# Norm column inside the mixers' first segment, and late weight splits queued behind the turned softmax tiles

## The chip, the cores and the metric

The kernel runs on one core of one Trainium2 chip. A core has five engines with a queue each: TensorE (PE; its weight loads are listed as PEld), VectorE (DVE), ScalarE (ACT), GpSimd (POOL) and SyncE (SP), whose queue only issues DMA here. An engine takes its instructions in the order in which they stand in its queue; instructions of different engines are held together by semaphores. The metric is the device time of one execution in microseconds (us). Before the change the median of three runs is 984.71 us (984.63 to 985.41).

## The reference: what is computed

A decoder trunk of two layers over 256 tokens of width 1024, all in float32. Each layer is a half SwiGLU step (FFN, inner width 2816), an attention mixer with 16 heads of 64, and another half SwiGLU step. Every step reads an RMS-normalised copy of the stream:

```python
y = xf * lax.rsqrt(jnp.mean(xf * xf, axis=-1, keepdims=True) + RMS_EPS)
return (y * g.astype(jnp.float32)).astype(x.dtype)
```

Mixer a projects q, k and v, rotates 16 of 64 columns of each q and k head, adds up three dilated window patterns (in the kernel one mask of logarithms of counts), and projects the result with `a_w_o`. Mixer b does causal attention with its own q projection and keys and values that were projected from another norm of the stream after layer 0; with 256 tokens there is a single block of keys. The output is a final RMS norm.

## The kernel before

**Precision.** Every float32 product is made of three products of float32r halves. A weight tile `raw` is rounded by ACT (`wh`) and the remainder is subtracted by DVE (`wl`); I call this pair a split. Splits are made for 128x1024 elements at a time, into pools of eight buffers; `raw` has four buffers, so a load on SP's queue waits until both halves of an older tile are split. Activations are split in the same manner (`parts_of`).

**Norms.** The stream lies transposed in `hT` (feature rows, token columns). A `Norm` makes two things. `scale` gives gain-scaled, split blocks `x`, which products can use at once. The factor per token comes later: `square` lets ACT square the eight blocks and POOL add them up in `ss`; `finish` sums over the partitions with four small PE products (`col`, L238), adds epsilon on DVE (`v`, L240) and takes the power -0.5 on POOL (`c`, L242). The result is one column per token tile (two tiles of 128 tokens), and it is applied when a projection leaves its accumulator.

**A mixer** (L704 to L786) works in segments. A segment is one block of 512 projected columns for both token tiles: for the first four weight rows tile 0 then tile 1, for the last four the same, three products for each row (L184, L186, L188). `evacuate` scales a finished accumulator by the norm's column (ACT, L752), lets DVE rotate it (L622 to L625) and, when q and k of a group of heads are there, has PE turn them (L741, `qt`). In mixer a the norm's column isn't there when the first segment ends; in mixer b the first segment (k and v) uses a norm whose column is long known, and the second (q) one whose column isn't. For those, both tiles are evacuated after the segment's last product:

```python
if norm.col is None:
    norm.finish()
    for t in range(NT):
        evacuate(i, t, norm.col[t], acs[t], parts)
```

Attention goes by pairs of heads, 0 to 7: scores (PE L643, DVE L651), softmax (ACT L657, POOL L664), turn of the softmax (PE L669 `pt`, split into `pT` by ACT L98 and DVE L94), values (PE L683 and L685 `po`), and evacuation of those (`o`, `oT`). The output projection (`out_t`, L580) multiplies with the pairs as they come: five rows in a main loop of 24 products each, the last three held back and done together at the end.

**Order.** A small agenda (L258) decides at which point of PE's work a step is written down: `after(wait, ...)` puts a step `wait` us of estimated work later. Weights of a mixer come through `Pieces` (L284): asking for one piece rounds all up to four pieces further on (`LEAD`), and DVE's subtraction is written one piece later. Finally the framework's scheduler sorts the queues by its own cost model, within the dependencies; so a split written down late can still be put early in ACT's and DVE's queues, whenever its raw tile and a free buffer are there by that model.

**The FFN after a mixer** loads its first unit of gate and up weights (1 MB each) as four splits, `wh_f_g` and `wh_f_u` (L158, L159). They need nothing of the mixer's result, so they stand among the mixer's last steps in the queues.

Of the kernel before, what the change touches and what calls it, by code (L numbers as in the profile page):

```python
# [29 lines left out]
LEAD = 4  # L30
# [36 lines left out]
def trunk(ctx: ExitStack, tc: tile.TileContext, a: dict, out: bass.AP):  # L67
    nc = tc.nc
# [69 lines left out]
    def late_constants():  # L138
        nc.sync.dma_start(rot, a["rot"].rearrange("t p c n -> p t c n"))
        nc.sync.dma_start(masks, a["masks"].rearrange("i p n -> p i n"))  # L140
        nc.sync.dma_start(gfin, a["final_norm"].rearrange("(o d) -> o d", o=1).to_broadcast([P, D]))


    def unit(name, k, n, srcs):

        raw = rawp.tile([P, k, n], F32, tag="raw", name=f"raw_{name}")
        for dst, src in srcs:
            nc.sync.dma_start(raw if dst is None else raw[:, :, dst], src)
        return pieces_of(name, raw, k, n)

    def pieces_of(name, raw, k, n):
        pieces = []
        for j in range(0, k, 1024 // n):
            kk = min(1024 // n, k - j)
            wh = wp.tile([P, kk, n], F32R, tag="wh", name=f"wh_{name}_{j}")
            wl = wp.tile([P, kk, n], F32R, tag="wl", name=f"wl_{name}_{j}")
            r = raw[:, j:j + kk, :]
            nc.scalar.activation(wh, r, AF.Copy)  # L158
            nc.vector.tensor_sub(wl, r, wh.bitcast(F32))  # L159
            for i in range(kk):  # L160
                pieces.append((wh[:, i, :], wl[:, i, :]))
        return pieces
# [15 lines left out]
    def rows(w, k0, k, c0, n):  # L178
        return w[k0 * P:(k0 + k) * P, c0:c0 + n].rearrange("(k p) n -> p k n", p=P)
# [104 lines left out]
    class Pieces:  # L284
# [29 lines left out]
                    self.rest.pop(0)()  # L314

        def __getitem__(self, i):
            self.split(i + LEAD)
            return self.parts[i]


# [16 lines left out]
        parts_of(hi, lo, flat(q), later=rest.append)  # L337
        return rest

    def ffn_blocks(name, wg, wu, norm, first=None, beside=(), sums=None):  # L340

        blocks, pairs, rest = [], {}, []

        def both(f, pair):
            acs = [acc(f"{name}_{n}{f}") for n in "gu"]
            cols = slice(f % 2 * P, (f % 2 + 1) * P)
            products_t(acs, [[(wh[:, cols], wl[:, cols]) for wh, wl in w] for w in pair], norm.x, True, True)
            return acs  # L350

        def close(f, gate, up):
            g = joined(gate, f"{name}_g{f}")
            nc.vector.tensor_mul(g, g, norm.row)  # L354
# [12 lines left out]
            parts_of(x[:, 0], x[:, 1], prod)  # L367
            while rest:
                rest.pop(0)()
            if prod is not g and f % 2:  # L370
                rest.extend(quarter_sums(pairs.pop(pair), *sums[pair], f"{name}_{f}"))
            blocks.append(x)

        done = []

        def close_all():
            if done and norm.row is None:
                norm.spread()
            for args in done:
                close(*args)  # L380
            done.clear()

        for f in range(0, KF, 2):
            if f == 0 and first is not None:
                ws = opening(wg, wu, first)
            else:
                ws = zip(*[unit(f"{name}_{n}{f}", KD, S, [(None, rows(w, 0, KD, f * P, S))])
                           for n, w in (("g", wg), ("u", wu))])
# [24 lines left out]
        return blocks  # L413
# [12 lines left out]
                                for j in range(2))  # L426
        return sums

    def ffn(name, layer, which, norm, after, first=None, beside=(), homes=("kx4", "kx6", "qkh", "qkh")):
        wg, wu, wd = (a[f"ffn{which}_w_{n}"][layer] for n in ("gate", "up", "down"))  # L430
        sums = left_sums(homes)
        blocks = ffn_blocks(name, wg, wu, norm, first, beside, sums)
        if which == 1:
            table(AF.Exp, blocks[-1][:, 0, 0:1].bitcast(F32))
        down(f"{name}_d", wd, blocks, sums, after)
# [141 lines left out]
                part(t, slice(512 + S, 1024), True)  # L577
            after(t)

    def out_t(name, pieces, base, blocks, norm, tail=3):  # L580

        accs = [acc(f"ot_{name}_{i}") for i in range(KD // 2)]

# [8 lines left out]
                nc.tensor.matmul(ac, wl[:, d], hi, start=False, stop=k == KD - 1 and j == 1)  # L592

        for k in range(KD - tail):
            ws = pieces[base + k][0]
            while len(blocks) <= k:
                yield None
            for i in range(KD // 2):
                step(i, k, ws)
                yield 0.72  # L600
# [26 lines left out]
    def attention(agenda, operands, mask, name, blocks):  # L627
# [38 lines left out]
        def turn(p, i):  # L666
            tr = trt(f"pt_{name}{p}_{i}")[:, :3 * P]
            for n in range(3):
                nc.tensor.transpose(tr[:, n * P:(n + 1) * P], sms[p, i][:, n * P:(n + 1) * P], ident)  # L669
            pT = pTs[p, i] = pp.tile([P, 2, 3 * P], F32R, tag="pT", name=f"pT_{name}{p}_{i}")  # L670
            parts_of(pT[:, 0], pT[:, 1], tr, later=agenda.soon)

        def values(p):
            g, b = divmod(p, HG // 2)
# [26 lines left out]

        return scores, turn, values

    def mixer(name, segs, plan, wo, mask, after):  # L704

# [17 lines left out]
        for norm in {id(norm): norm for norm, _, _ in segs}.values():  # L723
            for i in range(len(norm.late)):
                agenda.after(1.5 + 0.5 * i, lambda norm=norm: norm.late.pop(0)())
        scores, turn, values = attention(agenda, lambda g: (qks[g], vss.get(g)), mask, name, blocks)

        def turns(p):
# [18 lines left out]
        def evacuate(i, t, r, ac, parts):  # L747
# [38 lines left out]
        agenda.run(out_t(f"{name}o", pieces, base, blocks, after))  # L786


    def first(k, n):
# [21 lines left out]
    def ending(at):  # L811
# [28 lines left out]
    blocks = ffn_blocks("f21", a["ffn2_w_gate"][1], a["ffn2_w_up"][1], n6, beside=[lambda: None] + turns, sums=sums)  # L840

    parts = [[], []]
    outs = [[None, None] for t in range(NT)]
# [63 lines left out]
```

## Time and profile before

| | |
|---|---|
| median of three runs | 984.71 us |
| the profiled execution | 984.39 us |
| its span, first to last instruction | 982.6 us |
| mean granted TensorE clock | 0.999 |
| busy: PE, DVE, ACT, POOL | 968.3, 813.0, 613.8, 289.6 us |
| mixer a in the span, about | 190 to 310 us |
| mixer b in the span, about | 675 to 790 us |

The profile's page gives busy time by engine. Other answers of the trace list instructions in order of time: start, length, engine, line, operation, output and inputs, size, count, and in brackets the idle time of the engine just before it and what ended that. Equal neighbours are merged into one row with their count; the ends of matmuls are modelled, so the next product can start before the last has ended in the list. Buffer numbers are left out of names: `wl_qka` stands for several tiles.

### The profile page before, as it was taken

What the parts mean: (1) busy time and instruction counts of PE and PEld (TensorE: products, weight loads), DVE (VectorE), ACT (ScalarE), POOL (GpSimd) and SP (SyncE); (2) the same over time, 40 slices, a digit from 0 to 9 for tenths busy, and PEclk for the clock granted to TensorE, in tenths of its full rate; (3) what the DMA queues carried; (4) which work ended last, traced back from release to release, by engine and by line L of the source; (5) the groups of instructions that cost most, each with busy time, mean ns of one, the idle gap of its engine ahead of it and who ended that gap; (6) DMA issues with size and microseconds to landing.
All of it is one profiled execution on the core that took longest, in us unless ns stands there. A gap on an engine that the chain in (4) does not pass through costs nothing.

```text
span 982.6 us, 14865 instructions
## 1 busy us (share of the span) xinstructions
PE 968.3 (99%) x5391; PEld 832.8 (85%) x5391; DVE 813.0 (83%) x1383; ACT 613.8 (62%) x1131; POOL 289.6 (29%) x242
## 2 busy tenths in 40 slices
PE   8999999999999999999999999999999999999997
PEld 6888888878889888888888888888788998888886
DVE  7988899887878788889898888987678778888995
ACT  7656657567776566556576655656577766666561
POOL 3211246132342211146032121612142422112461
PEclk9999999999999999999999999999999999999999
DMA  9876636664443565545755555483744345565351
GB/s 317 256 238 186 197 132 217 223 203 155 132 129 106 179 201 178 185 158 210 256 168 176 172 182 205 171 283 109 248 131 129 101 158 170 177 204 180 129 171 43
DMA packets 126857, 176.00 MB, mean 179 GB/s; under 512 B 3392, under 2 KB 106304, under 8 KB 126784
## 3 DMA queue, kind: packets, MB, share of 16 engines
q1 hardware_dynamic: 125936, 174.01, 54.4%
q10 hardware_dynamic: 848, 1.05, 0.3%
q8 instruction: 42, 0.69, 0.3%
q14 instruction: 31, 0.25, 0.1%
HBM read 173.99 MB, written 1.05 MB: 178 GB/s over the span
## 4 chain that ended last, share of the span: by engine, by line
PE 68%; ACT 2%; DVE 2%; issue 1%; POOL 0%; POOLq 0%; ACTq 0%; DVEq 0%
PE f_g L195 12%; PE f_u L195 12%; PE f_u L198 6%; PE f_g L198 6%; PE dn_f_d L188 5%; PE dn_f_d L186 5%; PE dn_f_d L184 5%; PE dn_f_d_m L188 1%; PE dn_f_d_m L186 1%; PE dn_f_d_m L184 1%; PE q_b L184 1%; PE q_b L188 1%; PE q_b L186 1%; PE ot_ao L592 1%; PE ot_ao L590 1%; PE kv_b L184 1%
## 5 line engine op out<-in xcount | busy, mean ns | idle before, releaser
L357 POOL TENSOR_TENSOR j_f_u<-j_f_u,r_n 128x256 f32<-128x256 f32 x88 | 92.3, 1051 | 360.9 <-DVE j_f_u L325 338.1
L195 PE MATMUL f_g<-x_n,wh_f_g 128*128 128x512 f32 x688 | 180.5, 394 | 0.0
L195 PE MATMUL f_u<-x_n,wh_f_u 128*128 128x512 f32 x688 | 177.2, 390 | 0.0
L195 PEld LDWEIGHTS f_u<-x_n,wh_f_u 128*128 128x128 f32 x688 | 129.2, 188 | 27.3
L195 PEld LDWEIGHTS f_g<-x_n,wh_f_g 128*128 128x128 f32 x688 | 124.0, 189 | 22.7
L159 DVE TENSOR_TENSOR wl_f_u<-raw_f_u,wh_f_u 128x1024 fp32r<-128x1024 f32 x86 | 113.1, 1317 | 2.7 <-ACT wh_f_u L158 2.7
L159 DVE TENSOR_TENSOR wl_f_g<-raw_f_g,wh_f_g 128x1024 fp32r<-128x1024 f32 x86 | 104.1, 1229 | 3.9 <-ACT wh_f_g L158 3.9
L198 PE MATMUL f_u<-x_n,wl_f_u 128*128 128x256 f32 x688 | 103.3, 283 | 0.0
L198 PE MATMUL f_g<-x_n,wl_f_g 128*128 128x256 f32 x688 | 102.7, 282 | 0.0
L198 PEld LDWEIGHTS f_g<-x_n,wl_f_g 128*128 128x128 f32 x688 | 96.4, 190 | 6.3
L158 ACT ACTIVATE wh_f_u<-raw_f_u 128x1024 fp32r<-128x1024 f32 x86 | 87.9, 1048 | 13.4 <-PE f_g L195 7.5
L158 ACT ACTIVATE wh_f_g<-raw_f_g 128x1024 fp32r<-128x1024 f32 x86 | 89.5, 1048 | 5.0 <-PE f_g L195 2.8
L198 PEld LDWEIGHTS f_u<-x_n,wl_f_u 128*128 128x128 f32 x688 | 91.6, 192 | 0.0
L355 ACT ACTIVATE j_f_g<-j_f_g 128x256 f32<-128x256 f32 x88 | 36.7, 417 | 87.2 <-DVE j_f_g L354 86.9
L233 POOL TENSOR_TENSOR ss_n<-ss_n,sq_n 128x256 f32<-128x256 f32 x42 | 38.4, 914 | 148.3 <-ACT sq_n L232 146.3
L98 ACT ACTIVATE act_f<-j_f_g 128x256 fp32r<-128x256 f32 x58 | 23.9, 418 | 56.6 <-DVE j_f_g L365 56.6
L365 DVE TENSOR_TENSOR j_f_g<-j_f_g,j_f_u 128x256 f32<-128x256 f32 x58 | 27.9, 487 | 30.1 <-POOL j_f_u L357 30.1
L473 POOL TENSOR_TENSOR sum_f_d_6b<-sum_f_d_6ac,raw_f_d 128x512 f32<-128x512 f32 x4 | 45.5, 11374 | 17.6 <-DVE sum_f_d_6ac L472 13.2
L325 DVE TENSOR_TENSOR j_f_g<-f_g,j_f_g 128x256 f32<-128x256 f32 x88 | 36.7, 417 | 11.9 <-ACT j_f_g L324 11.9
L664 POOL TENSOR_SCALAR sm_b<-sm_b,ls_b 128x128 f32<-128x128 f32 (+1 forms) x32 | 29.8, 949 | 44.0 <-DVE ls_b L662 34.3
L664 POOL TENSOR_SCALAR sm_a<-sm_a,ls_a 128x128 f32<-128x128 f32 (+1 forms) x32 | 28.0, 890 | 50.0 <-DVE ls_a L662 32.8
L324 ACT ACTIVATE j_f_u<-f_u 128x256 f32<-128x256 f32 x88 | 33.0, 375 | 14.7 <-PE row_n L250 13.7
(565 smaller groups left out, 2386.5 us busy)
## 6 DMA issues: line engine op xcount, KB each, us to landing
raw_f_d<-in_ffn_w_down_dram SPq DMA_DIRECT2D x44, 1024.0 KB, 5.0
raw_f_g<-in_ffn_w_gate_dram SPq DMA_DIRECT2D x43, 1024.0 KB, 5.4
raw_f_u<-in_ffn_w_up_dram SPq DMA_DIRECT2D x43, 1024.0 KB, 5.4
raw_qka<-in_a_w_qkv_dram SPq DMA_DIRECT2D x16, 512.0 KB, 4.9
raw_va<-in_a_w_qkv_dram SPq DMA_DIRECT2D x4, 1024.0 KB, 6.0
raw_ao<-in_a_w_o_dram SPq DMA_DIRECT2D x4, 1024.0 KB, 4.9
raw_kvb<-in_kv_w_dram SPq DMA_DIRECT2D x8, 512.0 KB, 4.4
raw_qb<-in_b_w_q_dram SPq DMA_DIRECT2D x4, 1024.0 KB, 5.5
```

The lines of the kernel that those rows point to most:

```text
L158: nc.scalar.activation(wh, r, AF.Copy)
L159: nc.vector.tensor_sub(wl, r, wh.bitcast(F32))
L184: nc.tensor.matmul(ac, xh, wh, start=first, stop=False)
L186: nc.tensor.matmul(ac, xh, wl, start=False, stop=False)
L188: nc.tensor.matmul(ac, xl, wh, start=False, stop=last)
L195: nc.tensor.matmul(ac, wh, flat(x), start=first and i == 0, stop=False)
L198: nc.tensor.matmul(ac[:, :S], wl, x[:, 0, :], start=False, stop=last and i == len(ws) - 1)
L233: nc.gpsimd.tensor_tensor(self.ss, self.ss, sq, op=ALU.add)
L325: nc.vector.tensor_add(s, ac[:, :S], s)
L357: nc.gpsimd.tensor_tensor(u, u, norm.row, op=ALU.mult)
L473: nc.gpsimd.tensor_tensor(b[:, 0], ac[:, 0], raw[:, 3], op=ALU.add)
L664: nc.gpsimd.tensor_scalar(sm[:, seg], sm[:, seg], ls[:, t:t + 1], None, op0=ALU.mult)
```

## The change

First, the norm's column. When a norm of a mixer has none yet, `finish` goes on the agenda at 8.1 us from the mixer's start, which is after tile 0's last product of the first segment and before tile 1's last twelve. Every token tile is then evacuated as soon as its own products are done, in mixer a's first segment and in mixer b's second. In a mixer's first segment the turn of q and k is written down 4.4 us after tile 0's evacuation and 3.2 us after tile 1's, in place of 3.2 for both.

Second, late splits. The framework's `issue_after` gives every instruction traced in a block an order behind a given instruction of the same engine. `marks[p]` keeps the rounding (ACT) and the subtraction (DVE) of head pair p's turned softmax, `pT`. The splits named in `queue` are placed behind the marks of the pair given there. In mixer a these are the splits asked for by the output projection's steps 3 and 4 (behind pairs 4 and 5) and the four of the next FFN's first unit (behind 5, 6, 7, 7); in mixer b the four of the next FFN (behind 4, 5, 6, 7). In the output projection's main loop a piece is now asked for with three pieces ahead, not four.

In the compiled queues this moves: on PE, four column products up by twelve products in mixer a and by more than a segment in mixer b, tile 0's `qt` turns two rows up in mixer a and four in mixer b, and mixer a's fifth value product together with its turns ahead of two output products; on ACT and DVE, the rotation and evacuation steps of the first heads between weight splits, and the late splits behind `pT`. GpSimd's and SyncE's queues keep their order. No instruction with work is added or taken away.

```diff
+    marks = {}
+    def queued(p):
+        stack = ExitStack()
+        for ins in marks.get(p, ()):
+            stack.enter_context(tc.issue_after(ins.ins))
+        return stack
...
-    def unit(name, k, n, srcs):
+    def unit(name, k, n, srcs, behind=()):
...
+        behind = iter(behind)
...
-            nc.scalar.activation(wh, r, AF.Copy)
-            nc.vector.tensor_sub(wl, r, wh.bitcast(F32))
+            with queued(next(behind, None)):
+                nc.scalar.activation(wh, r, AF.Copy)
+                nc.vector.tensor_sub(wl, r, wh.bitcast(F32))
...
         def __getitem__(self, i):
-            self.split(i + LEAD)
+            return self.get(i)
+
+        def get(self, i, lead=LEAD):
+            self.split(i + lead)
             return self.parts[i]
...
         for k in range(KD - tail):
-            ws = pieces[base + k][0]
+            with queued(queue.get(k)):
+                ws = pieces.get(base + k, 3)[0]
...
-            parts_of(pT[:, 0], pT[:, 1], tr, later=agenda.soon)
+            hi = nc.scalar.activation(pT[:, 0], tr, AF.Copy)
+            def rest():
+                marks[p] = [hi, nc.vector.tensor_sub(pT[:, 1], tr, pT[:, 0].bitcast(F32))]
+            agenda.soon(rest)
...
+            if norm.col is None:
+                agenda.after(8.1, norm.finish)
...
-                    agenda.after(3.2, turn_in, g, t)
+                    agenda.after(4.4 - 1.2 * t if i == 0 else 3.2, turn_in, g, t)
...
-                        if k0 + 4 == KD and norm.col is not None:
+                        if k0 + 4 == KD:
                             evacuate(i, t, norm.col[t], acs[t], parts)
-                if norm.col is None:
-                    norm.finish()
-                    for t in range(NT):
-                        evacuate(i, t, norm.col[t], acs[t], parts)
...
-          a["a_w_o"][0], masks[:, 0, :], n2)
-    ffn("f20", 0, 2, n2, n3)
+          a["a_w_o"][0], masks[:, 0, :], n2, {3: 4, 4: 5})
+    ffn("f20", 0, 2, n2, n3, queue=(5, 6, 7, 7))
...
+                        queue=(4, 5, 6, 7))
```

More of the change, by code (lines that the diff above doesn't have):

```diff
@@ L148, in unit @@
             nc.sync.dma_start(raw if dst is None else raw[:, :, dst], src)
-        return pieces_of(name, raw, k, n)
-    def pieces_of(name, raw, k, n):
         pieces = []
+        behind = iter(behind)
         for j in range(0, k, 1024 // n):
@@ L338, in quarter_sums, with ffn_blocks @@
         return rest
-    def ffn_blocks(name, wg, wu, norm, first=None, beside=(), sums=None):
+    def ffn_blocks(name, wg, wu, norm, first=None, beside=(), sums=None, queue=()):
         blocks, pairs, rest = [], {}, []
@@ L386, in ffn_blocks @@
             else:
-                ws = zip(*[unit(f"{name}_{n}{f}", KD, S, [(None, rows(w, 0, KD, f * P, S))])
-                           for n, w in (("g", wg), ("u", wu))])
+                ws = zip(*[unit(f"{name}_{n}{f}", KD, S, [(None, rows(w, 0, KD, f * P, S))], behind[:2 if f == 0 else 0])
+                           for n, w, behind in (("g", wg, queue[:2]), ("u", wu, queue[2:]))])
             if f == 0:
@@ L427, in left_sums, with ffn @@
         return sums
-    def ffn(name, layer, which, norm, after, first=None, beside=(), homes=("kx4", "kx6", "qkh", "qkh")):
+    def ffn(name, layer, which, norm, after, first=None, beside=(), homes=("kx4", "kx6", "qkh", "qkh"), queue=()):
         wg, wu, wd = (a[f"ffn{which}_w_{n}"][layer] for n in ("gate", "up", "down"))
         sums = left_sums(homes)
-        blocks = ffn_blocks(name, wg, wu, norm, first, beside, sums)
+        blocks = ffn_blocks(name, wg, wu, norm, first, beside, sums, queue)
         if which == 1:
@@ L578, in down_last, with out_t @@
             after(t)
-    def out_t(name, pieces, base, blocks, norm, tail=3):
+    def out_t(name, pieces, base, blocks, norm, queue, tail=3):
         accs = [acc(f"ot_{name}_{i}") for i in range(KD // 2)]
@@ L702, in attention, with mixer @@
         return scores, turn, values
-    def mixer(name, segs, plan, wo, mask, after):
+    def mixer(name, segs, plan, wo, mask, after, queue={}):
         n = HG * DH
@@ L777, in projections @@
                             yield 0.68
-                        if k0 + 4 == KD and norm.col is not None:
+                        if k0 + 4 == KD:
                             evacuate(i, t, norm.col[t], acs[t], parts)
-                if norm.col is None:
-                    norm.finish()
-                    for t in range(NT):
-                        evacuate(i, t, norm.col[t], acs[t], parts)
         agenda.run(projections())
-        agenda.run(out_t(f"{name}o", pieces, base, blocks, after))
+        agenda.run(out_t(f"{name}o", pieces, base, blocks, after, queue))
     def first(k, n):
@@ L839, in trunk @@
     turns = [lambda t=t, c=c: turn_h(t, c) for t in range(NT) for c in range(2)]
-    blocks = ffn_blocks("f21", a["ffn2_w_gate"][1], a["ffn2_w_up"][1], n6, beside=[lambda: None] + turns, sums=sums)
+    blocks = ffn_blocks("f21", a["ffn2_w_gate"][1], a["ffn2_w_up"][1], n6, beside=[lambda: None] + turns, sums=sums,
+                        queue=(4, 5, 6, 7))
     parts = [[], []]
```

## Prediction

> **What bounds the kernel now.** I read the page's busy shares first, then the busy time of the two mixer stretches, then TensorE's instructions in order of time, looking for starts that came late.
>
> ```profile
> PE 968.3 (99%) x5391; PEld 832.8 (85%) x5391; DVE 813.0 (83%) x1383; ACT 613.8 (62%) x1131; POOL 289.6 (29%) x242
> ```
>
> TensorE (PE) is busy 968.3 of 982.6 us, and the change neither adds nor removes a product. All it can win or lose is idle time of PE, 14.3 us in the whole span. The columns of the next rows are stretch, length, then busy us (instructions) of PE, PEld, DVE, ACT, POOL.
>
> ```profile
> 190.00:305.00 115.00, 111.89 (x694) 94.56 (x693) 89.86 (x212) 80.90 (x173) 35.56 (x40) 1.00 0.46 147
> 672.00:787.00 115.00, 112.85 (x692) 95.67 (x691) 91.37 (x222) 82.24 (x180) 38.43 (x40) 1.00 0.44 144
> ```
>
> The mixers hold 3.1 and 2.2 us of PE idle. It sits in five places (start, us, instruction, and in brackets the idle time before it and what ended it):
>
> ```profile
> 208.46 1.23 PE L741 MATMUL qt_a<-ident,rt_a 128*128 128x128 f32 x8 [1.65 <-DVE rt_a L625]
> ...
> 283.98 0.36 PE L683 MATMUL po_a<-pT_a,vs_a 128*128 128x256 f32 x1 [0.79 <-DVE vs_a L96]
> ...
> 285.57 0.39 PE L683 MATMUL po_a<-pT_a,vs_a 128*128 128x256 f32 x1 [0.67 <-DVE pT_a L94]
> ...
> 702.60 1.22 PE L741 MATMUL qt_b<-ident,rt_b 128*128 128x128 f32 x8 [1.04 <-DVE rt_b L625]
> ...
> 770.12 0.38 PE L683 MATMUL po_b<-pT_b,vs_b 128*128 128x256 f32 x1 [0.97 <-DVE pT_b L94]
> ```
>
> Two are the turn of the first heads, waiting for the rotation; three are attention's value products, waiting for VectorE (DVE). The change touches both places in both mixers, so there are four terms.
>
> **Term 1, mixer a's first segment.** PE's column products (L238) move ahead of the second token tile's last twelve products; tile 0 is evacuated twelve products earlier; its turn moves two weight rows (six products) up, tile 1's stays where it was.
>
> ```profile
> 200.02 0.40 PE L184 MATMUL qk_a<-wh_qka,x_n 128*128 128x512 f32 x1
> ...
> 202.76 0.50 PE L238 MATMUL col_n<-mean,ss_n 128*128 128x1 f32 x4
> 203.12 0.47 PE L184 MATMUL v_a<-wh_va,x_n 128*128 128x512 f32 x1
> ...
> 209.44 0.47 PE L184 MATMUL v_a<-wh_va,x_n 128*128 128x512 f32 x1
> ```
>
> ```profile
> 195.78 4.45 POOL L233 TENSOR_TENSOR ss_n<-ss_n,sq_n 128x256 f32<-128x256 f32 x4 [3.86 <-ACT sq_n L232]
> 204.87 1.62 POOL L242 TENSOR_TENSOR c_n<-v_n,expo 128x2 f32<-128x2 f32 x1 [4.64 <-DVE v_n L240]
> ```
>
> ```profile
> 201.23 3.48 DVE L312 TENSOR_TENSOR wl_qka<-raw_qka,wh_qka 128x1024 fp32r<-128x1024 f32 x3
> 204.64 0.15 DVE L240 TENSOR_SCALAR v_n<-col_n 128x2 f32<-128x2 f32 x1
> 204.71 1.21 DVE L312 TENSOR_TENSOR wl_qka<-raw_qka,wh_qka 128x1024 fp32r<-128x1024 f32 x1
> 207.25 0.29 DVE L622 TENSOR_TENSOR ra_a<-rt_a,rot 128x128 f32<-128x128 f32 x1 [1.33 <-ACT rt_a L752]
> ...
> 208.03 0.28 DVE L625 TENSOR_TENSOR rt_a<-ra_a,rb_a 128x128 f32<-128x128 f32 x1
> ...
> 208.62 0.29 DVE L625 TENSOR_TENSOR rt_a<-ra_a,rb_a 128x128 f32<-128x128 f32 x1
> ```
>
> ```profile
> 206.53 1.27 ACT L752 ACTIVATE rt_a<-qk_a,c_n 128x512 f32<-128x512 f32 x2 [2.51 <-POOL c_n L242]
> ```
>
> *A new wait.* The column is now due on PE at 200.02, but GpSimd's last sum of squares ends at 195.78 + 4.45 = 200.23. A hand-over to PE takes 0.15 (rotation ends 208.03 + 0.28 = 208.31, PE starts 208.46), so the column starts at 200.38: 0.36 lost, with tile 1's twelve products queued behind it though nothing holds them. The column's own 0.36 (202.76 to 203.12) only moves. The v products start at 203.48; nine of them at 0.23 ((202.76 - 200.02) / 12) put tile 0's turn at 205.6.
>
> *The chain to that turn.* `v_n` now stands behind the first of three weight subtractions: 201.23 + 3.48/3 = 202.39. From its start to `rt_a` took 206.53 - 204.64 = 1.89, so 204.28; 0.72 to the rotation (207.25); four DVE steps without the other tile between them about 0.88; 0.15 to PE: 206.03, a wait of 0.43. Then four turns (0.44 of the 0.98 that eight took to 209.44) and six products: 207.9. Tile 1's evacuation stands behind a weight rounding on ScalarE (ACT, 1.06) and its rotation behind a subtraction (1.2): 204.28 + 0.64 + 1.0 + 0.1 + 1.2 + 0.88 + 0.15 = 208.25, a wait of 0.35. Four turns more and the next v product starts at 208.69, not 209.44. **Gain 0.75**; bounds -0.4 (only the new wait counts) and 1.9 (209.44 - 208.46 - 0.88 + 1.65 + 0.16, all old waiting gone). I take the chain, which is made of rows.
>
> What decides here is `c_n`: 1.62 with a subtraction beside it, while the shortest of six took 0.72.
>
> ```profile
> L242 POOL TENSOR_TENSOR c_n<-v_n,expo x6: 718/800/1778, 20.9 to 805.7; 128x2 f32<-128x2 f32 x6
> ```
>
> The subtraction at 204.71 began 0.16 before `c_n` and kept its 1.21; `c_n` took the loss. In the new order a ready subtraction follows `v_n` again, so I keep 1.62. The Trainium skill, SBUF — State Buffer, section "SBUF: two separate sides", says that a VectorE operation with two SBUF inputs and a GpSimd operation exclude each other for a whole instruction, the first one winning; by that rule 1.62 recurs, and the rows agree. Were `c_n` to take its free 0.72, both turn waits (0.43 and 0.35) would go and the sum below would be 4.7.
>
> **Term 2, mixer b.** The column moves from after the second segment into the first, so that q is evacuated tile by tile as it is done.
>
> ```profile
> 680.13 4.45 POOL L233 TENSOR_TENSOR ss_n<-ss_n,sq_n 128x256 f32<-128x256 f32 x4 [3.85 <-ACT sq_n L232]
> ```
>
> ```profile
> 683.89 0.39 PE L184 MATMUL kv_b<-wh_kvb,x_kx 128*128 128x512 f32 x1
> ...
> 703.58 0.47 PE L184 MATMUL kv_b<-wh_kvb,x_kx 128*128 128x512 f32 x1
> ```
>
> Due at 683.89, the column waits until 680.13 + 4.45 + 0.15 = 684.73: 0.84 lost. The old wait goes: 1.04, 0.16 for breaking PE's flow (a product booked at 0.39 is followed after 0.23), 0.1 between the two turns (703.58 - 702.60 - 0.88), 1.3 in all. Tile 0 is ready 2.74 earlier than now and its turn comes three products after q's end, with 0.7 + 2.74 to go by and a chain of 0.2 + 0.72 + 0.88 + 0.15 = 1.95; tile 1 has one subtraction (1.2) more in its chain and four more rows of three products to wait in. **Gain 0.5**, between -0.84 and 1.3.
>
> **Term 3, mixer a's values.** Late roundings and subtractions of the output weights and of the next FFN's first unit go behind the softmax's turned tiles.
>
> ```profile
> 282.91 0.28 PE L592 MATMUL ot_ao<-oT_a,wl_ao 128*128 128x256 f32 x1
> ...
> 289.40 0.40 PE L683 MATMUL po_a<-pT_a,vs_a 128*128 128x256 f32 x2
> ...
> 290.28 0.84 PE L669 MATMUL pt_a<-ident,sm_a 128*128 128x128 f32 x6
> ...
> 293.12 0.40 PE L683 MATMUL po_a<-pT_a,vs_a 128*128 128x256 f32 x2
> ```
>
> ```profile
> 280.74 1.04 ACT L310 ACTIVATE wh_ao<-raw_ao 128x1024 fp32r<-128x1024 f32 x1
> 281.69 0.81 ACT L98 ACTIVATE vs_a<-v_a,c_n 128x256 fp32r<-128x256 f32 x2
> ```
>
> ```profile
> 281.82 1.23 DVE L312 TENSOR_TENSOR wl_ao<-raw_ao,wh_ao 128x1024 fp32r<-128x1024 f32 x1 [0.79 <-ACT wh_ao L310]
> ...
> 284.97 1.01 DVE L94 TENSOR_TENSOR pT_a<-pt_a,pT_a 128x384 fp32r<-128x384 f32 x2
> ...
> 291.29 0.85 DVE L692 TENSOR_TENSOR o_a<-po_a,o_a 64x256 f32<-64x256 f32 x2 [0.21 <-ACT o_a L687]
> 292.17 1.02 DVE L94 TENSOR_TENSOR pT_a<-pt_a,pT_a 128x384 fp32r<-128x384 f32 x2
> 293.11 0.42 DVE L94 TENSOR_TENSOR oT_a<-o_a,oT_a 128x256 fp32r<-128x256 f32 x1
> ```
>
> ACT's `vs_a` loses the rounding before it and starts at 280.74, DVE's the subtraction at 281.82, and the low half of `pT_a` (284.97) another: 280.74 + 0.81 on ACT, 0.8 for DVE's part of `vs_a` and 0.56 for half of `pT` end at 282.9. So head pair 4's values start at 283.03 (282.91 + 0.12), unhindered. The next pair follows after the products (289.40 to 290.28, 0.88), turns and eighteen output products (to 293.12, 2.84) and six more (0.74): 287.49 in place of 289.40, 1.91 won. Then DVE is late. From a pair's first product to its `o_a` sum takes 291.29 - 289.40 = 1.89, so 284.92; in its new queue follow `o_a` 0.88, `pT` 0.94, a subtraction 1.14, `oT` 0.38, two subtractions 2.28, `o_a` 0.88 and half of `pT` 0.56: 291.98, at PE 292.13. Pair 6 is due at 287.49 + 3.72 = 291.21 and its second product at 291.33: 0.8 lost. **Gain 1.1**, between 0.3 (twice that wait) and 1.9.
>
> **Term 4, mixer b's values.** Only the FFN's four splits move.
>
> ```profile
> 767.30 1.04 ACT L158 ACTIVATE wh_f_g<-raw_f_g 128x1024 fp32r<-128x1024 f32 x1
> ```
>
> ```profile
> 768.77 0.38 PE L683 MATMUL po_b<-pT_b,vs_b 128*128 128x256 f32 x1
> ...
> 778.27 0.64 PE L683 MATMUL po_b<-pT_b,vs_b 128*128 128x256 f32 x2
> ```
>
> Without the rounding at 767.30 `pT_b` is rounded there, its low half is done near 768.4, and the second product follows the first (768.77) after 0.12: 770.12 - 768.89 = 1.23 won. With the splits in wider gaps the pair at 778.27 (0.64 where 289.40 has 0.40) gives 0.24 more. The chain 1.89 + 0.88 + 0.56 + 0.15 = 3.48 fits the 3.7 or more between pairs when no subtraction stands in it, as here. **Gain 1.5**, between 0.5 and 1.5.
>
> **Costed at nothing:** the FFNs' first units, split later. What hides them is the three held blocks, 72 products of 0.12 = 8.6 us, after the last split; without that cover each split costs ACT 1.06 and DVE 1.2. The next unit's loads on SP's queue wait for a raw buffer that mixer a frees later (the subtraction of the sixth output row now follows `pT`); that unit's products come after the held blocks and the FFN's first unit, so I price it at nothing too. The smaller lead changes no order beyond this; no DMA is added.
>
> **Sum:** 0.75 + 0.5 + 1.1 + 1.5 = 3.9 us. The profiled execution took 984.39 (span 982.6 and 1.8 around it), so 980.5; the median of the runs, 984.71, is 0.3 higher, so 980.8.
>
> **Rivals.**
> *All waits vanish* (the hand-overs are shorter, sums finish sooner): 1.9 + 1.3 + 1.9 + 1.5 = 6.6, so 978.1. For it: my estimates stack every latency; against it: the ends 200.23 and 684.58 are later than PE's arrival by rows that the change does not touch. 12%.
> *Waits only move:* both first segments give nothing and pair 6 of mixer a takes twice its wait: 0.3 + 1.5 = 1.8, so 982.9. For it: DVE is busy 90 of 115 us in these stretches. 14%.
> *Slower:* the column at the head of PE's in-order queue. It used to come 2.5 us after the last sum of squares (202.76 against 200.23); now each us by which that sum is late stops PE twice. If each of the last four adds takes double (8.9 for 4.45), PE loses 4.45 more in each mixer: 984.7 + 8.9 - 3.9 = 989.7. It decides from 2 us per mixer. Against it: nothing ahead of those adds changes. 5%.
>
> **How the numbers follow.** Likeliest, 69%: 980.8, by itself 979.6 to 982.2. The range reaches to near the first two rivals, 978.6 to 983.1. A measurement can tell about 0.2% (2 us) from no change: below 982.7 is faster. The likeliest and the first rival lie there, and a little of the second: 82% faster, 12% same, 6% slower (the third and what I overlooked).
>
> **What would show it.** In the new profile PE should wait for `ss_n` before the column, about 0.4 at the first mixer and 0.8 at the second; twice about 0.4 before `qt_a`; not before `qt_b`; not at pair 4 of either mixer, but about 0.8 for `pT_a` at mixer a's pair 6. `c_n` should stay near 1.6 in mixer a. Wrong would be: a wait before the FFNs' first products, a column wait over 1 us, or PE waits in the mixers adding up to more than 4 us.

## The result, and the profile after

The changed kernel takes 980.14 us (median of six runs, 980.05 to 980.23) against 984.62 us before (six runs, 984.36 to 985.41): a ratio of 0.9954, with a 95% interval of 0.9941 to 0.9967. That is faster by 0.46%. The prediction was 980.8 us with a range of 978.6 to 983.1. The profiled execution took 980.13 us with a span of 978.4 (before: 984.39 and 982.6).

The busy time of the two mixer stretches of the changed kernel, in the columns of the prediction's second view (stretch, length, then busy us and instructions of PE, PEld, DVE, ACT, POOL):

```profile
190.00:305.00 115.00, 114.24 (x711) 96.49 (x710) 91.56 (x217) 81.55 (x177) 34.65 (x40) 1.00 0.45 147
672.00:787.00 115.00, 114.30 (x717) 97.91 (x716) 92.37 (x226) 82.69 (x182) 36.99 (x41) 1.00 0.44 147
```

PE's idle time in them fell from 3.1 and 2.2 us to 0.8 and 0.7. TensorE's instructions of the changed kernel in order of time, at the places that the prediction named:

```profile
200.04 0.61 PE L246 MATMUL col_n<-mean,ss_n 128*128 128x1 f32 x4
...
205.76 0.63 PE L761 MATMUL qt_a<-ident,rt_a 128*128 128x128 f32 x4 [0.23 <-ACT wh_qka L318]
...
207.95 0.63 PE L761 MATMUL qt_a<-ident,rt_a 128*128 128x128 f32 x4 [0.18 <-DVE rt_a L638]
208.34 0.47 PE L192 MATMUL v_a<-wh_va,x_n 128*128 128x512 f32 x1
...
281.89 0.28 PE L604 MATMUL ot_ao<-oT_a,wl_ao 128*128 128x256 f32 x1
282.01 0.40 PE L701 MATMUL po_a<-pT_a,vs_a 128*128 128x256 f32 x2
...
286.43 0.40 PE L701 MATMUL po_a<-pT_a,vs_a 128*128 128x256 f32 x2
...
290.43 0.88 PE L701 MATMUL po_a<-pT_a,vs_a 128*128 128x256 f32 x2
...
295.36 0.40 PE L701 MATMUL po_a<-pT_a,vs_a 128*128 128x256 f32 x2
...
682.41 0.61 PE L246 MATMUL col_n<-mean,ss_n 128*128 128x1 f32 x4 [0.57 <-POOL ss_n L241]
...
700.83 0.48 PE L192 MATMUL kv_b<-wh_kvb,x_kx 128*128 128x512 f32 x1
...
766.09 0.40 PE L701 MATMUL po_b<-pT_b,vs_b 128*128 128x256 f32 x2
...
778.68 0.40 PE L701 MATMUL po_b<-pT_b,vs_b 128*128 128x256 f32 x2
```

Two rows of the kernel before are wanted beside them, the last value products of each mixer:

```profile
297.58 0.40 PE L683 MATMUL po_a<-pT_a,vs_a 128*128 128x256 f32 x2
...
782.94 0.40 PE L683 MATMUL po_b<-pT_b,vs_b 128*128 128x256 f32 x2
```

**How to read a wait from starts.** The brackets understate small waits, because a matmul's end is modelled: the product ahead of the column at 200.04 is listed into its start, so no bracket stands there. I therefore go by starts. PE's pace is 0.23 from start to start for a 512-wide product and 0.12 for a 256-wide one; what a start is later than that is called "late" below. In the changed kernel these starts are late: the column by 0.37 and 0.73, the two turns of mixer a by 0.38 and 0.34, pair 6 of mixer a by 0.28, and the product behind its first two by 0.48. One more is late in mixer b, the second of two score products, and it is so by the same amount in the kernel before (762.39, 0.73):

```profile
759.73 0.73 PE L656 MATMUL s_b<-qkh_b 64*128 64x128 f32 x2
```

The two at 756.52 take 0.33; here the second product starts at 760.14, about 0.35 late, and the trace puts that down to DVE's reading of older scores (L664). The change doesn't touch it. No other place in the mixers is late by more than 0.21. The two `qt_b` turns, pair 4 of both mixers and the first products of the FFNs behind them don't wait.

**Where the time went, by PE's starts.** How far the changed kernel is ahead of the one before, from pairs of rows (those of before stand in the prediction or above):

| place | before | after | ahead by |
|---|---|---|---|
| behind mixer a's first turns | 209.44 | 208.34 | 1.10 |
| ahead of pair 4, mixer a | 282.91 | 281.89 | 1.02 |
| pair 7, mixer a | 297.58 | 295.36 | 2.22 |
| where the column is due, mixer b | 683.89 | 681.68 (682.41 - 0.73) | 2.21 |
| behind the first turns, mixer b | 703.58 | 700.83 | 2.75 |
| pair 4's first product, mixer b | 768.77 | 766.09 | 2.68 |
| pair 7, mixer b | 782.94 | 778.68 | 4.26 |

The four terms are differences of these: 1.10, of which 0.22 was there before mixer a began (next section), so 0.88; 2.22 - 1.02 = 1.20; 2.75 - 2.21 = 0.54; 4.26 - 2.68 = 1.58. Between them 0.16 was lost in small pieces.

### The profile page after: what moved, and what is told of

It is laid out like the page before. It is cut to its first block, busy times and chain, and to the rows that moved or that the text cites. A ratio compares the mean times of both kernels' runs of the same rounds, so it can differ in the third digit from the quotient of the medians.

```text
span 978.4 us, 14860 instructions
## 1 busy us (share of the span) xinstructions
PE 967.5 (99%) x5391; PEld 831.9 (85%) x5391; DVE 813.0 (83%) x1383; ACT 612.7 (63%) x1131; POOL 287.0 (29%) x242
## 4 chain that ended last, share of the span: by engine, by line
PE 92%; DVE 4%; ACT 2%; issue 1%; POOL 1%; DMA 0%; SPq 0%; POOLq 0%; DVEq 0%; ACTq 0%
PE f_g L203 16%; PE f_u L203 16%; PE f_u L206 8%; PE f_g L206 8%; PE dn_f_d L196 6%; PE dn_f_d L192 6%; PE dn_f_d L194 6%; PE dn_f_d_m L196 1%; PE dn_f_d_m L194 1%; PE dn_f_d_m L192 1%; PE qk_a L192 1%; PE qk_a L196 1%; PE qk_a L194 1%; DVE x_n L96 1%; PE q_b L192 1%
## 5 line engine op out<-in xcount | busy, mean ns | idle before, releaser
L365 DVE TENSOR_TENSOR j_f_g<-j_f_g,r_n 128x256 f32<-128x256 f32 x88 | 41.4, 474 | 0.7
```

## The experiments

Each of them is an edit of the changed kernel; the diffs are cut to the lines that matter. All are compared by TensorE's starts, by the median, and by the profiled execution's own time.

**A common offset first.** The profiled executions differ by some tenths before any mixer begins. In the kernel's first 18 us PE waits for the first weights; the last of those waits in the changed kernel:

```profile
17.28 0.38 PE L206 MATMUL f_g<-x_n,wl 128*128 128x256 f32 x1 [0.81 <-DVE wl L182]
```

This start lies between 17.05 and 17.70 in the twelve profiles, and none of the edits touches anything ahead of it. So the table has a column in which each profiled execution is moved to a start of 17.28: its time less (start - 17.28). By that column before is 984.17 and after 980.13, a difference of 4.04. Ratios are to the kernel before in the same comparison, whose medians were 984.68 for e1 to e4, 984.51 for e5 to e8 and 984.89 for e9 and e10. The intervals of the ratios reach 0.9 to 1.3 us to either side, so differences of less than that between two edits rest on the profiled executions, one of each kernel, and on TensorE's starts in them, not on the ratios.

| kernel | median (lowest to highest), us | ratio to before, 95% | profiled | start | moved to 17.28 |
|---|---|---|---|---|---|
| before | 984.62 (984.36 to 985.41) | | 984.39 | 17.50 | 984.17 |
| after | 980.14 (980.05 to 980.23) | 0.9941 to 0.9967 | 980.13 | 17.28 | 980.13 |
| e1 splits only | 981.56 (981.40 to 982.22) | 0.9953 to 0.9978 | 981.62 | 17.45 | 981.45 |
| e2 column only | 983.13 (982.72 to 984.74) | 0.9975 to 0.9993 | 983.13 | 17.40 | 983.01 |
| e3 pair 6, one less | 979.65 (979.49 to 980.01) | 0.9932 to 0.9959 | 979.59 | 17.49 | 979.38 |
| e4 pair 6, ACT only | 980.36 (980.04 to 980.88) | 0.9940 to 0.9965 | 980.57 | 17.70 | 980.15 |
| e5 rotation first | 979.71 (979.68 to 980.17) | 0.9939 to 0.9964 | 979.69 | 17.67 | 979.30 |
| e6 column later | 980.87 (980.52 to 981.40) | 0.9950 to 0.9975 | 980.87 | 17.66 | 980.49 |
| e7 both | 978.91 (978.51 to 980.41) | 0.9933 to 0.9960 | 978.51 | 17.05 | 978.74 |
| e8 all | 978.15 (978.09 to 979.06) | 0.9924 to 0.9949 | 978.15 | 17.44 | 977.99 |
| e9 column earlier | 980.96 (980.72 to 981.07) | 0.9945 to 0.9972 | 980.72 | 17.24 | 980.76 |
| e10 all and pair 0 | 977.75 (977.62 to 978.32) | 0.9914 to 0.9939 | 977.62 | 17.45 | 977.45 |

### Each half alone

The first run takes the column and the evacuation back to where they were:

```diff
-            if norm.col is None:
-                agenda.after(8.1, norm.finish)
...
-                    agenda.after(4.4 - 1.2 * t if i == 0 else 3.2, turn_in, g, t)
+                    agenda.after(3.2, turn_in, g, t)
...
-                        if k0 + 4 == KD:
+                        if k0 + 4 == KD and norm.col is not None:
                             evacuate(i, t, norm.col[t], acs[t], parts)
+                if norm.col is None:
+                    norm.finish()
+                    for t in range(NT):
+                        evacuate(i, t, norm.col[t], acs[t], parts)
```

> The column and the evacuation are put back to where they stood before; only the queueing of late splits behind the turned probabilities stays (and the lead of 3 for the output weights). Theory (four places, each lost or won for itself): only the value products of both mixers gain, 1.2 + 1.6 = 2.8 us, so 981.8; the waits of 1.65 and 1.04 before the first qt_a and qt_b are back, the column waits on nothing. Rival (the parts feed each other: an earlier segment lets the later stages run ahead, or the queued splits need the earlier start): the gain is clearly off 2.8, below 2.2 or above 3.4.

Its TensorE rows show the two old waits again:

```profile
208.39 1.22 PE L759 MATMUL qt_a<-ident,rt_a 128*128 128x128 f32 x8 [1.62 <-DVE rt_a L638]
...
701.33 1.22 PE L759 MATMUL qt_b<-ident,rt_b 128*128 128x128 f32 x8 [1.04 <-DVE rt_b L638]
```

The second run keeps the column and takes the queueing out:

```diff
-                ws = pieces.get(base + k, 3)[0]
+                ws = pieces[base + k][0]
...
-          a["a_w_o"][0], masks[:, 0, :], n2, {3: 4, 4: 5})
-    ffn("f20", 0, 2, n2, n3, queue=(5, 6, 7, 7))
+          a["a_w_o"][0], masks[:, 0, :], n2)
+    ffn("f20", 0, 2, n2, n3)
...
-                        queue=(4, 5, 6, 7))
```

> The other half alone: the column inside the first segment with evacuation tile by tile, and no split queued (lead 4 as before). Theory (separate places): 0.9 + 0.55 = 1.4 us gained, so 983.2; PE waits before po_a at pair 4 (0.79 and 0.67) and before po_b (0.97) are as before, pair 6 of mixer a has none. Together with the run of the other half the gains make the whole, 4.2 to 4.5. Rival (the parts feed each other): the two gains do not add up, short or over by more than 0.5.

Its TensorE rows show a wait at each mixer's pair 4:

```profile
283.08 0.36 PE L701 MATMUL po_a<-pT_a,vs_a 128*128 128x256 f32 x1 [0.81 <-DVE vs_a L96]
...
768.83 0.39 PE L701 MATMUL po_b<-pT_b,vs_b 128*128 128x256 f32 x1 [0.97 <-DVE pT_b L687]
```

By the table's last column the splits alone win 984.17 - 981.45 = 2.72 and the column alone 984.17 - 983.01 = 1.16. Together 3.88, and the whole change wins 4.04. Medians say 3.12 and 1.55 (before had a median of 984.68 in that comparison), together 4.67 against 4.48. Either way they add up within 0.2, as separate places should; the rival that the parts feed each other by more than 0.5 falls.

### What makes pair 6 of mixer a wait

The prediction put that wait down to one subtraction too many in DVE's queue. VectorE's instructions of the changed kernel ahead of pair 6:

```profile
287.17 1.22 DVE L320 TENSOR_TENSOR wl_ao<-raw_ao,wh_ao 128x1024 fp32r<-128x1024 f32 x1
288.31 1.22 DVE L167 TENSOR_TENSOR wl_f_g<-raw_f_g,wh_f_g 128x1024 fp32r<-128x1024 f32 x1
289.44 0.84 DVE L710 TENSOR_TENSOR o_a<-po_a,o_a 64x256 f32<-64x256 f32 x2
290.31 1.02 DVE L687 TENSOR_TENSOR pT_a<-pt_a,pT_a 128x384 fp32r<-128x384 f32 x2
```

The third run queues the first of the FFN's splits behind pair 6:

```diff
-    ffn("f20", 0, 2, n2, n3, queue=(5, 6, 7, 7))
+    ffn("f20", 0, 2, n2, n3, queue=(6, 6, 7, 7))
```

> The first split of the FFN's unit is queued behind pair 6 rather than pair 5: one rounding on ACT and one subtraction on DVE (1.14 net) leave the stretch between pair 5's oT and pair 6's pT. Theory (DVE's in-order queue between two pairs holds three subtractions, one too many): pair 6's wait, 0.28 + 0.48 = 0.76, goes, 979.4. Rival (the pair waits for its turned probabilities from PE or ACT, whatever DVE does): 980.1. Rival (the subtraction only moves the wait to pair 7, where two now stand): pair 7 waits 0.5 or more and the time stays near 980.

VectorE, then TensorE, in that run:

```profile
287.33 1.22 DVE L320 TENSOR_TENSOR wl_ao<-raw_ao,wh_ao 128x1024 fp32r<-128x1024 f32 x1
288.47 0.85 DVE L710 TENSOR_TENSOR o_a<-po_a,o_a 64x256 f32<-64x256 f32 x2
289.35 1.02 DVE L687 TENSOR_TENSOR pT_a<-pt_a,pT_a 128x384 fp32r<-128x384 f32 x2
```

```profile
290.30 0.40 PE L701 MATMUL po_a<-pT_a,vs_a 128*128 128x256 f32 x2
```

Without `wl_f_g` between them, `pT` starts 2.02 after the start of that `wl_ao` in place of 3.14, which is one subtraction less, and the first two products of pair 6 take 0.40 in place of 0.88. Nothing is late at pair 6 or pair 7. The time is 979.38 against 980.13, 0.75 less, where the two late starts were 0.76 together.

The fourth run changes ACT's order alone, by queueing the second split behind pair 5 as well:

```diff
-    ffn("f20", 0, 2, n2, n3, queue=(5, 6, 7, 7))
+    ffn("f20", 0, 2, n2, n3, queue=(5, 5, 7, 7))
```

> The second split of the FFN's unit is queued behind pair 5 as well; in the order only ACT changes: its rounding (1.06) now stands ahead of pair 5's o_a copy and of pair 6's pT rounding; DVE's queue is the same. Theory (DVE decides at pair 6, and ACT has 0.56 idle before that copy and 0.3 to spare until DVE reaches it): no change, 980.1, pair 6's wait 0.76 to 0.9. Rival (ACT's roundings ahead of pT make the wait): about 1 us more, 981.1.

ScalarE, then TensorE, in that run:

```profile
286.35 2.00 ACT L166 ACTIVATE wh_f_g<-raw_f_g 128x1024 fp32r<-128x1024 f32 x2
```

```profile
290.88 0.88 PE L701 MATMUL po_a<-pT_a,vs_a 128*128 128x256 f32 x2
```

Two roundings now stand in a row ahead of pair 5's copy, and pair 6 is late by the same 0.28 and 0.48 (its start of 290.88 is 290.43 moved by the common offset). 980.15 against 980.13: ACT doesn't decide there, DVE does.

### What makes the two turns of mixer a wait

VectorE, then GpSimd, in the changed kernel around the column:

```profile
199.31 1.75 DVE L320 TENSOR_TENSOR wl_va<-raw_va,wh_va 128x1024 fp32r<-128x1024 f32 x1
200.99 1.21 DVE L320 TENSOR_TENSOR wl_qka<-raw_qka,wh_qka 128x1024 fp32r<-128x1024 f32 x1
202.12 0.15 DVE L248 TENSOR_SCALAR v_n<-col_n 128x2 f32<-128x2 f32 x1
202.19 1.21 DVE L320 TENSOR_TENSOR wl_qka<-raw_qka,wh_qka 128x1024 fp32r<-128x1024 f32 x1
```

```profile
195.55 4.43 POOL L241 TENSOR_TENSOR ss_n<-ss_n,sq_n 128x256 f32<-128x256 f32 x4 [3.85 <-ACT sq_n L240]
202.35 1.62 POOL L250 TENSOR_TENSOR c_n<-v_n,expo 128x2 f32<-128x2 f32 x1 [2.37 <-DVE v_n L248]
```

The column is done on PE by 200.65 (200.04 + 0.61), `v_n` starts at 202.12 behind a subtraction, and `c_n` takes 1.62 beside the next. The fifth run queues the four subtractions of the third segment's unit behind `v_n` and both rotations; on the other engines nothing moves:

```diff
+            marks["first"] = [nc.vector.tensor_scalar_add(v, ps[:, :NT], EPS)]
...
+        marks["first"] = [nc.vector.tensor_add(v[:, :, :ROT], ta, tb)]
...
+                def lower(wl=wl, raw=raw, wh=wh, name=name):
+                    with queued("first" if name.startswith("qka2") else None):
+                        nc.vector.tensor_sub(wl, raw, wh.bitcast(F32))
```

> In mixer a the four weight subtractions of the third segment's unit are queued on DVE behind the column's factor and the rotations of both tiles; nothing else moves. v_n can then start at about 201.1 instead of 202.12, and no subtraction runs beside c_n. Theory (one: DVE's queue makes both turn waits; two: c_n takes 1.62 because of the subtraction beside it): both waits before qt_a, 0.38 and 0.34, go, 979.4; c_n takes 0.7 to 0.8. Rival to the second: c_n stays near 1.6 with nothing beside it (a slow first use of pow on GpSimd there); the waits go all the same, since v_n alone is 1 us earlier. Rival to the first (PE or ACT hold the turns): waits stay, 980.1. What could be late instead: the third segment's products, if the subtractions, some 4 us later, are not done by then (about 214).

VectorE, GpSimd and TensorE in that run:

```profile
199.70 1.75 DVE L323 TENSOR_TENSOR wl_va<-raw_va,wh_va 128x1024 fp32r<-128x1024 f32 x1
201.38 0.15 DVE L248 TENSOR_SCALAR v_n<-col_n 128x2 f32<-128x2 f32 x1
```

```profile
195.94 4.43 POOL L241 TENSOR_TENSOR ss_n<-ss_n,sq_n 128x256 f32<-128x256 f32 x4 [3.86 <-ACT sq_n L240]
201.60 0.71 POOL L250 TENSOR_TENSOR c_n<-v_n,expo 128x2 f32<-128x2 f32 x1 [1.23 <-DVE v_n L248]
```

```profile
205.77 0.60 PE L766 MATMUL qt_a<-ident,rt_a 128*128 128x128 f32 x4
...
207.59 0.60 PE L766 MATMUL qt_a<-ident,rt_a 128*128 128x128 f32 x4
```

`c_n` takes 0.71, both turns follow without a wait, and the third segment's products aren't late either. 979.30, 0.83 less, where the two waits were 0.72. So `c_n`'s 1.62 is the work of the subtraction beside it, not of the place: the same operation takes 0.71 when VectorE has nothing to do, and 1.63 in the sixth run below, where a subtraction stands beside it again.

### Moving the column

The sixth run has the column one weight row later, and tile 0's evacuation right behind it:

```diff
-                agenda.after(8.1, norm.finish)
+                agenda.after(8.8, norm.finish)
...
+        def done(i, t):
+            norm, x, parts = segs[i]
+            if norm.col is None:
+                agenda.after(0.65, done, i, t)
+            else:
+                evacuate(i, t, norm.col[t], kept[i][t], parts)
...
-                            evacuate(i, t, norm.col[t], acs[t], parts)
+                            done(i, t)
```

> The column comes one weight row (three products, 0.69) later in both mixers, and the first tile is evacuated right behind it; DVE's order then has v_n behind two subtractions in mixer a instead of one, and behind one more in mixer b. Theory (the column only stands in front of PE because it is early, and what it releases is held by DVE's queue): the waits before col_n, 0.37 and 0.73, shrink to 0 to 0.1, and v_n comes 1.2 later in mixer a, so the waits before qt_a grow by about as much: 979.6 to 980.6, no clear gain. Rival (the column's wait is the whole price, the rest has slack): 979.1.

VectorE, then TensorE, in that run:

```profile
201.38 2.35 DVE L320 TENSOR_TENSOR wl_qka<-raw_qka,wh_qka 128x1024 fp32r<-128x1024 f32 x2
203.65 0.14 DVE L248 TENSOR_SCALAR v_n<-col_n 128x2 f32<-128x2 f32 x1
```

```profile
207.47 0.63 PE L761 MATMUL qt_a<-ident,rt_a 128*128 128x128 f32 x4 [1.21 <-DVE rt_a L638]
...
209.35 0.63 PE L761 MATMUL qt_a<-ident,rt_a 128*128 128x128 f32 x4 [0.56 <-DVE rt_a L638]
```

The column waits no longer in either mixer, which wins 0.37 and 0.73; but `v_n` now stands behind two subtractions, and the turns are late by 1.36 and 0.72 in place of 0.38 and 0.34, which loses 1.36. Net a loss of 0.26; the table's last column says 980.49 - 980.13 = 0.36, within what was expected (the median, 980.87, is above it, with a start of 17.66). A wait that was removed came back one step down the chain, larger.

The seventh run makes both edits, with the turns written down at `3.8 - 0.6 * t` so that they keep their place:

> The two edits before together: column one weight row later, and in mixer a its factor and both rotations ahead of the third segment's subtractions. Theory: with DVE's queue out of the way the later column costs nothing, and all four waits go (0.37 + 0.38 + 0.34 + 0.66): 978.4. Rival (the later column takes what the rotation's earlier place gave): no better than the rotation alone, 979.4.

978.74 (expected 978.4), 1.39 less than the changed kernel, where the four late starts were 1.82; all four are gone. What is missing is a new one, 0.41 in mixer a's pair 0, which the eighth run shows too:

> As the run before, and the first split of the FFN's unit behind pair 6 instead of pair 5, as in the third run. Theory (every remaining wait is for itself): 978.4 - 0.7 = 977.7, and PE waits on nothing over 0.3 in either mixer's stretch. Rival (the waits feed each other): not under 978.2.

977.99 (expected 977.7), and the 0.41 is over the 0.3 that was expected as the most. VectorE and TensorE there:

```profile
223.35 1.24 DVE L323 TENSOR_TENSOR wl_qka<-raw_qka,wh_qka 128x1024 fp32r<-128x1024 f32 x1 [0.78 <-ACT wh_qka L318]
224.52 1.01 DVE L692 TENSOR_TENSOR pT_a<-pt_a,pT_a 128x384 fp32r<-128x384 f32 x2
```

```profile
224.70 0.81 PE L706 MATMUL po_a<-pT_a,vs_a 128*128 128x256 f32 x2
```

The pattern is that of pair 6: a subtraction ahead of `pT`, and the products behind it take 0.81 in place of 0.40. PE reaches pair 0 0.98 earlier than in the changed kernel (224.70 for 225.68), DVE's `pT` only 0.24 (224.52 for 224.76). The tenth run queues that one subtraction behind pair 0's `pT` (the diff is against the eighth run):

```diff
-                    with queued("first" if name.startswith("qka2") else None):
+                    with queued("first" if name.startswith("qka2") else 0 if name == "qka4_0" else None):
```

> As the run with all edits, and one subtraction of the fifth segment's weights on DVE queued behind the turned probabilities of mixer a's pair 0 (in that run it ran at 223.35 for 1.24, ahead of pT at 224.52, and the second of pair 0's products came 0.41 late). Theory (the same pattern as at pair 6: one subtraction ahead of pT): the 0.41 goes, 977.75, and no start in the mixers is late by more than 0.25. Rival (pT waits for its high half from ACT, 223.23 + 0.84, or for the turns): the 0.41 stays, 978.15.

The mixer stretches of that run, and the products of pair 0:

```profile
190.00:305.00 115.00, 115.00 (x727) 98.44 (x726) 92.42 (x220) 82.68 (x181) 33.55 (x42) 1.00 0.44 147
672.00:787.00 115.00, 114.86 (x729) 98.91 (x728) 92.89 (x228) 83.04 (x183) 36.16 (x41) 1.00 0.44 147
```

```profile
224.72 0.40 PE L706 MATMUL po_a<-pT_a,vs_a 128*128 128x256 f32 x2
```

PE is listed as idle for 0.14 us in 230, and the 0.41 at pair 0 is gone. The score products of mixer b are still about 0.36 late (757.22, 0.74 for two), against an expected 0.25 at most. By the table's last column the run is 0.54 below the eighth, 0.13 more than the wait; what the rest is stays open. The median is 977.75 us, as expected, a ratio to before of 0.9927 (0.9914 to 0.9939). It is the fastest kernel here, 2.4 us (0.24%) below the changed kernel by their medians, which come from separate comparisons.

The ninth run goes the other way, the column one row earlier:

```diff
-                agenda.after(8.1, norm.finish)
+                agenda.after(7.4, norm.finish)
```

> The column one weight row (three products, 0.69) earlier than in the changed kernel, in both mixers; only its place on PE moves, every other queue is the same. Its start is held by the last sum of squares, so PE should wait 0.69 longer before it: about 1.06 in mixer a, 1.42 in mixer b. Theory (in mixer a the chain from v_n to the turns starts at the same time and absorbs what PE arrives later: the wait before the first qt_a goes, that before the second shrinks to about 0): nothing lost in mixer a, 0.69 lost in mixer b, 980.8. Rival (each us of the column's wait costs a us in either mixer): 981.5. Rival (the sums are ahead by then, the wait does not grow): 980.1.

TensorE there:

```profile
199.99 0.61 PE L246 MATMUL col_n<-mean,ss_n 128*128 128x1 f32 x4 [0.96 <-POOL ss_n L241]
...
206.01 0.60 PE L761 MATMUL qt_a<-ident,rt_a 128*128 128x128 f32 x4
...
207.91 0.63 PE L761 MATMUL qt_a<-ident,rt_a 128*128 128x128 f32 x4
...
682.30 0.61 PE L246 MATMUL col_n<-mean,ss_n 128*128 128x1 f32 x4 [1.27 <-POOL ss_n L241]
```

The column starts where it did, held by the sum, and PE is idle before it for longer: late by 1.23 and 1.42. In mixer a the turns then need no wait, so the second one comes at 207.91 as before (207.95) and nothing is lost; mixer b, which had no wait behind the column, loses all of it. 980.76 against 980.13: 0.63, where one row is 0.69. The rival of 981.5 falls by these starts; the median, 980.96, lies between the two.

## Why the prediction was right, point by point

**What bounds the kernel.** Right. PE does the same products; all that was won is PE's idle time in the mixers, at the five places that the prediction listed. A sixth late start, the score products of mixer b, isn't in that list, since the listing shows no idle time before it; it is the same before and after.

**Term 1** (0.75; measured 0.88). The new wait before the column came out at 0.37 for 0.36. In part that is luck: the hand-over took 0.06 where 0.15 was reckoned (see term 2), while PE was ready for the column at 199.67 (200.04 - 0.37), which is 199.89 in the time of before and 0.13 ahead of the 200.02 that was taken, and the two nearly cancel. Both turn waits came as predicted, 0.38 for 0.43 and 0.34 for 0.35, and `c_n`'s 1.62 too. By the rule of the Trainium skill that was weighed there (SBUF — State Buffer, section "SBUF: two separate sides") it was to recur; it did, and the fifth run shows the other side of it, 0.71 without the subtraction. What remains, 0.13, are steps of a few hundredths each in a long chain.

**Term 2** (0.5; measured 0.54). The column's wait was 0.73 for 0.84. The step that was off is the hand-over from GpSimd to PE: I took 0.15 from a hand-over between VectorE and PE, and the rows give 200.04 - (195.55 + 4.43) = 0.06. No wait stood before `qt_b`, as predicted. All waits in the mixers come to 2.58 us, or 2.93 with the score products, under the 4 that would have spoken against the prediction.

**Term 3** (1.1; measured 1.20). In the time of before, pair 4 came at 282.01 + 1.02 = 283.03 (predicted 283.03), pair 5 at 286.43 + 1.02 = 287.45 (287.49), and pair 6 lost 0.76 (0.8). The third and fourth run show that the cause was the one named, DVE's queue with three subtractions ahead of `pT`. One detail was not predicted: 0.28 of the 0.76 comes before pair 6's first product. DVE's `o_a` of pair 5 ends at 289.44 + 0.84 = 290.28, 0.15 before it, so the accumulator that this frees is the likely cause; no run tells that apart from `pT`, since the third run moves both.

**Term 4** (1.5; measured 1.58), and **what was costed at nothing**: no FFN's first product is late, and the lead of 2.22 at pair 7 is still 2.21 in mixer b, so the FFN units between them cost nothing.

**The sum.** The terms came to 4.20 for 3.85. The profiled execution was forecast at 980.5 and took 980.13; of the difference 0.35 is the terms and 0.22 the first 18 us, less 0.16 lost in small pieces. For the median I added 0.3, by which the median of before was above its profile; after's median is 0.01 above its own. That step was wrong, and is half of the 0.66 between 980.8 and 980.14.

**The rivals.** *All waits vanish* (978.1) didn't happen, since the waits that the prediction kept are real; but its time is nearly that of the tenth run, 977.75, in which the subtractions and the column were moved so that none of these waits is left. *Waits only move* (982.9) fell; in small it is what the sixth run does. *Slower* fell: GpSimd's last sums took 4.43 for 4.45. The ninth run prices an early column, not a late sum: there a row of 0.69 costs about its length in mixer b and nothing in mixer a, where the chain to the turns absorbs it. Whether a later sum would stop PE in both, as the prediction had it, wasn't tried.

## What to carry to other kernels

When one engine is 99% busy, list its late starts, follow each back to the one instruction that stands too early in another engine's queue, and move that instruction behind the one that is waited for: here such moves cost no work, and the gains added up one by one, but for one wait that appeared anew (pair 0) and took a move of its own. Before a step is moved earlier, ask what it stands in front of and what stands in front of its successor: a column one row later won 1.10 at its own place and lost 1.36 two steps on, until the subtractions behind it were moved as well. In the ninth run a wait that had slack behind it cost nothing, and one without cost its full length, so the same edit can be free in one stage and dear in the next.

## What the runs showed of the hardware

The exclusion between VectorE and GpSimd works in the other direction too, which I had not reckoned with. The subtraction `wl_va` takes 1.75 in the changed kernel, where its like takes 1.21: it starts at 199.31 while GpSimd's last sum of squares runs, which ends at 195.55 + 4.43 = 199.98, and it ends 1.08 after that (201.06). In the fifth run it starts at 199.70, the sum ends at 200.37, and the subtraction at 201.45, again 1.08 after. And `c_n` ends at 203.97, 0.57 after the subtraction of 202.19 has ended. Both look as if the second to start got next to nothing done until the first had ended: 0.57 of its free 0.71 was left then, and 1.08 of its free 1.21. By the Trainium skill (SBUF — State Buffer, section "SBUF: two separate sides") whichever starts first holds the port pair for its whole instruction, which fits both directions. So a step that depends on a small GpSimd instruction, or stands behind a long one in VectorE's queue, pays for its neighbour: `v_n` of the fifth run starts at 201.38, right behind the stretched subtraction.

The same thing stands ahead of the column's own wait, which the prediction took as fixed. Of GpSimd's last four sums in the changed kernel the first takes much longer than the next, 0.81 from 197.42:

```profile
195.55 1.80 POOL L241 TENSOR_TENSOR ss_n<-ss_n,sq_n 128x256 f32<-128x256 f32 x1 [3.85 <-ACT sq_n L240]
```

A subtraction `wl_va` starts at 195.53 and ends at 195.53 + 1.22 = 196.75, and the sum ends 0.60 after it. Mixer b has the same, 1.80 from 677.91 behind a subtraction `wl_qb` from 677.90. That is about 1.0 us in each mixer, more than the 0.37 and 0.73 for which PE waits there. Whether those waits go when that subtraction is queued behind the sum wasn't tried.
